# A causal convolution's taps held in program order, fewer of them among the projections, and a normalization row one chunk later

## The chip, the cores and the metric

The kernel runs on one core of a Trainium2 chip. The metric is the device time in microseconds (us) of one execution, lower is better. A core has five engines that run their own instruction streams and wait for each other by semaphores: PE (TensorE, matmuls), DVE (VectorE), ACT (ScalarE), POOL (GpSimd) and SP (SyncE, which here only issues DMAs).

## What is computed

A hybrid decoder layer for 256 tokens of width 1024, all in float32: a convolution branch and a sparse-attention branch share one input projection and one output projection; after them come a cross-attention to a memory of 256 tokens, a mixture of 16384 tiny experts chosen by product keys, and a final norm. Cut to what this change touches:

```python
def conformer_conv(a, b, w_dw, b_dw, ln_g, ln_b):
    u = a * jax.nn.sigmoid(b)
    y = lax.conv_general_dilated(      # depthwise, causal, CONV_KERNEL = 31 taps, 512 channels
        u, w_dw[:, None, :], window_strides=(1,), padding=[(CONV_KERNEL - 1, 0)], ...)
    y = layernorm(y + b_dw, ln_g, ln_b)
    return jax.nn.silu(y)

hn = rmsnorm(h, mix_norm_g[l])
proj = hn @ w_in[l]
conv_a, conv_b, q, k_c, v_c, k_s, v_s, k_w, v_w, gate_logits = jnp.split(proj, IN_SPLITS, axis=-1)
y_conv = conformer_conv(conv_a, conv_b, ...)
y_nsa = nsa_mixer(q, k_c, v_c, k_s, v_s, k_w, v_w, gate_logits, ...)
h = h + jnp.concatenate([y_conv, y_nsa], axis=-1) @ w_out[l]
```

## The kernel before

Activations lie transposed, features on 128 partitions and the 256 tokens along the free dimension. A weight chunk of 128 output features is one 512 KB DMA (`raw`, four buffers), which ACT rounds to a coarse part `hi` and DVE turns into a rest `lo` (line 138, two halves of 512 columns, six buffers of each). `proj` then does three matmuls for each of the eight blocks of 128 input features (lines 148 to 150): 24 matmuls of 256 columns for a chunk.

The start of the program is a chain of such chunks: four pairs `pb`, `pa` for the convolution's gate and value (`i` from 0 to 3), two `pkv`, six `pq`, and four double chunks `pv` that hold the values and gates. Before a projection can be used it has to be multiplied by the first norm's row `rs_x`: `r0.sums()` adds squares on PE and DVE takes the reciprocal root, `r0.rows()` spreads it over the partitions by a matmul (`sr_x`, line 224) that ACT copies. `conv_in(i, ...)` forms the gated input `u` of channel group `i` and puts that group's 31 taps on a list; `conv(n)` takes up to `n` of them off it and issues them. A tap is one DVE instruction that adds `u`, shifted by `j`, times a weight to `yc` (line 273; `j` = 0 is line 271): 124 taps in all, and within a group each reads what the last one wrote.

After the projections PE runs the memory's key and value projections as filler, first with the small network that compresses keys (`ph`), then between the 16 units of attention (loop over `n` from 0 to 17). A unit `n` is: scores `pss` on PE, row maximum `amx` on DVE (line 562), exponential on ACT, scaling on DVE, and two units later transposes on PE. Behind the transposes of each `n` stands `conv(6)`. At `n` = 12 `ln_mean()` issues what taps are left and adds the four groups (`lsum`, lines 610 to 613); at `n` = 13 `ln_center` has PE spread the sum (`pmu`, line 619); at 15 and 16 the layernorm's own reciprocal root follows (`ss_c`, `sr_c`). The first two chunks of the output projection are split around there too.

What sets the order: PE's stream is written by hand (`manual_schedule`), so it runs in the order of the code and a matmul that waits holds up all that stand behind it. The streams of DVE, ACT, POOL and SP are ordered by the framework's scheduler at build time, by readiness and place in the program; on the chip each engine then runs its stream strictly in that order.

Of the kernel before, what the change touches and what calls it, by code (L numbers as in the profile page):

```python
# [16 lines left out]
ALU = mybir.AluOpType  # L17
# [4 lines left out]
T = 256  # L22
D = 1024
KC = 8
# [68 lines left out]
def build(tc, A, out, dbg=None):  # L93
    nc = tc.nc
    V, S, G, PE = nc.vector, nc.scalar, nc.gpsimd, nc.tensor
# [17 lines left out]
    def Pm(name):  # L113
        return par[:, PC[name][0]:PC[name][1]]
# [5 lines left out]
    def wload(src, n=1024):  # L120
        cnt[0] += 1
        raw = wts.tile([P, 1024], F32, name=f"raw{cnt[0]}", tag="raw", bufs=4)
        if cnt[0] == 1:
            nc.sync.dma_start(raw[:, 0:512], src[:, 0:512])
            nc.sync.dma_start(raw[:, 512:], src[:, 512:])
        else:
            nc.sync.dma_start(raw[:, 0:n], src)
        return raw, cnt[0]

    def wsplit(w, engs=None, width=P, half=512):  # L130
        raw, i = w
        out_ = []
        for q in range(2):
            hi = wts.tile([P, 512], F32R, name=f"hi{i}{q}", tag="hi", bufs=6)[:, 0:half]
            lo = wts.tile([P, 512], F32R, name=f"lo{i}{q}", tag="lo", bufs=6)[:, 0:half]
            r = raw[:, half * q:half * q + half]
            S.activation(hi, r, AF.Copy)  # L137
            (engs or (V, V))[q].tensor_sub(lo, r, hi.bitcast(F32))  # L138
            for j in range(half // width):
                out_.append((hi[:, j * width:(j + 1) * width], lo[:, j * width:(j + 1) * width]))  # L140
        return out_

    def wchunk(src, engs=None, width=P):

        return wsplit(wload(src), engs, width)

    def mm3(ps, w, xh, xl, start, stop):
        PE.matmul(ps, w[0], xh, start=start, stop=False)  # L148
        PE.matmul(ps, w[0], xl, start=False, stop=False)  # L149
        PE.matmul(ps, w[1], xh, start=False, stop=stop)  # L150

    def proj(ps, w, x, ks=range(KC)):
        for k in ks:
            mm3(ps, w[k], x[0][:, k], x[1][:, k], k == 0, k == KC - 1)
# [20 lines left out]
    def psum(w, name, tag="mm"):  # L175
        return pm.tile([P, 512], F32, name=name, tag=tag, bufs=4)[:, :w]
# [70 lines left out]
    hx = (hx_h, hx_l)  # L247
# [11 lines left out]
    u = ch.tile([P, 4, 30 + T], F32, name="u")  # L259
    V.memset(u[:, :, 0:30], 0.0)  # L260
    yc = ch.tile([P, 4, T], F32, name="yc")
    taps = []

    def conv(n):
        for _ in range(min(n, len(taps))):
            taps.pop(0)()

    def tap(i, j):
        w = Pm("conv_w")[:, i * TAPS + j:i * TAPS + j + 1]
        if j == 0:  # L270
            V.tensor_scalar(yc[:, i], u[:, i, 0:T], w, Pm("conv_b")[:, i:i + 1], op0=ALU.mult, op1=ALU.add)
        else:
            V.scalar_tensor_tensor(yc[:, i], u[:, i, j:j + T], w, yc[:, i], op0=ALU.mult, op1=ALU.add)  # L273

    def conv_in(i, pb, pa):
        tb = wk.tile([P, T], F32, name=f"tb{i}", tag="tb")
        V.tensor_mul(tb, pb, r0.row)
        th = wk.tile([P, T], F32, name=f"th{i}", tag="th")
        S.activation(th, tb, AF.Tanh, scale=0.5)
        ta = wk.tile([P, T], F32, name=f"ta{i}", tag="ta")  # L280
        V.scalar_tensor_tensor(ta, pa, 0.5, r0.row, op0=ALU.mult, op1=ALU.mult)
        V.scalar_tensor_tensor(u[:, i, 30:], th, 1.0, ta, op0=ALU.add, op1=ALU.mult)
        for j in range(TAPS):
            taps.append(lambda j=j: tap(i, j))

    pend = []
    for i in range(4):
        pb = psum(T, f"pb{i}")
        wb = wchunk(A["w_in_t"][2 * i]) if i else w0
        proj(pb, wb, hx, range(4))  # L290
        if i == 1:
            r0.sums()
        proj(pb, wb, hx, range(4, KC))
        wa = wchunk(A["w_in_t"][2 * i + 1], None)
        if i == 0:
            for k in range(KC):
                r0.add(xT[:, k])
            nc.sync.dma_start(con1, A["con"][:, 0:NCON1])
        pa = psum(T, f"pa{i}")
        proj(pa, wa, hx, range(6))  # L300
        if i == 1:
            r0.rows()
            conv_in(*pend)
        proj(pa, wa, hx, range(6, KC))
        if i == 0:
            pend = (i, pb, pa)
        else:
            conv_in(i, pb, pa)
        conv(6)
    nc.sync.dma_start(con2, A["con"][:, NCON1:])  # L310
    posi = wk.tile([P, T], I32, name="posi", tag="rt")
    nc.sync.dma_start(posi, A["pos"].partition_broadcast(P))
# [31 lines left out]
    for i in range(2):  # L344
        G.memset(KV[i], 0.0)
        ps = psum(T, f"pkv{i}")
        proj(ps, wchunk(A["w_in_t"][8 + i]), hx)
        kvT = wk.tile([P, T], F32, name=f"kvT{i}", tag="kvT")
        V.tensor_mul(kvT, ps, r0.row)
        kt = KV[i]  # L350
        S.activation(kt[0:64, 0, 0:T], kvT[0:64, :], AF.Copy)
        S.activation(kt[64:128, 1, 0:T - 1], kvT[64:128, 1:T], AF.Copy)
        nc.sync.dma_start(kt[64:128, 0, 0:T - 1], kvT[0:64, 1:T])
        nc.sync.dma_start(kt[0:64, 1, 0:T], kvT[64:128, :])
        V.tensor_copy(kt[:, 2, 0:32:2], Pm("cmp_pos")[:, 16 * i:16 * i + 16])
        conv(3)
    nc.sync.dma_start(w2, A["w2"])

    w1 = [mp.tile([P, 16, P], F32, name=f"w1_{i}", tag=f"w1_{i}") for i in range(2)]
# [17 lines left out]
    def rope(i, src):  # L377
        pp_ = psum(T, f"rp{i}", "at")
        PE.matmul(pp_, C("perm"), src, start=True, stop=True)
        t = wk.tile([P, T], F32, name=f"rt{i}", tag="rt")  # L380
        V.tensor_mul(t, src, Ct)
        t2 = wk.tile([P, T], F32, name=f"ru{i}", tag="ta")
        V.tensor_mul(t2, pp_, St)
        V.tensor_add(t, t, t2)
        show(f"rope{i}", t)
        dh, dl = (k_h[:, i], k_l[:, i]) if i < 2 else (q_h[:, i - 2], q_l[:, i - 2])
        S.activation(dh, t, AF.Copy)
        V.tensor_sub(dl, t, dh.bitcast(F32))

    todo = []  # L390
    for i in range(6):
        dst = kraw[i] if i < 2 else qraw[:, i - 2]
        ps = psum(T, f"pq{i}")
        proj(ps, wchunk(A["w_in_t"][10 + i]), hx)
        V.tensor_mul(dst, ps, r0.row)
        if i >= 2:
            nc.sync.dma_start(w1[i // 2 - 1][:, 8 * (i % 2):8 * (i % 2) + 8], A["w1"][i // 2 - 1, :, 8 * (i % 2):8 * (i % 2) + 8])
        if i == 1:
            rm.sums()
        todo.append((i, dst))  # L400
        if i > 1:
            rope(*todo.pop(0))
        conv(3)


    vn = ch.tile([P, 2, 256], F32, name="vn")
# [1 line left out]
    for w in range(4):  # L408
        wc = wsplit(wload(A["w_in_v"][w], 560), (V, V), 280, 280)
        for j in range(2):  # L410
            k = 2 * w + j
            for hf in range(2):
                sl = slice(hf * P, (hf + 1) * P)
                PE.matmul(pv[hf], hx_h[:, k, sl], wc[j][0], start=(k == 0), stop=False)
                PE.matmul(pv[hf], hx_h[:, k, sl], wc[j][1], start=False, stop=False)
                PE.matmul(pv[hf], hx_l[:, k, sl], wc[j][0], start=False, stop=(k == KC - 1))
        if w % 2:
            rope(*todo[w // 2])
        if w == 1:
            rm.rows()  # L420
        conv(3)
    gate = ch.tile([P, 2, 8, 3], F32, name="gate")
    chalf = wk.tile([P, 2], F32, name="chalf", tag="bcol")
    V.tensor_scalar(chalf, r0.col, 0.5, None, op0=ALU.mult)
# [40 lines left out]
    def fill(n):  # L465
        for _ in range(n):
            if next(fl, 0) == 0:
                return
# [166 lines left out]
    for n in range(18):  # L635
        if n < 16:
            scores(*units[n])
        if n == 17:
            wc0 = wchunk(A["w_out"][0])
        fill(7 if n < 4 else 5 if n < 14 else 6)  # L640
        if n == 0:
            cmp_keys()
        if n == 1:
            cmp_values()
            cmp_scores(0)
        if n == 2:
            cmp_scores(1)
            prs = psum(512, "prsel", "at")
            for k in range(4):
                PE.matmul(prs[:, k * P:(k + 1) * P], C("rsel")[0:64, k * P:(k + 1) * P], vc2, start=True, stop=True)  # L650
            V.tensor_copy(vcp, prs.rearrange("p (a b) -> p a b", a=4))
        if n in (4, 5):
            cmp_transpose(n - 4)
        if n >= 6 and (n - 6) % 4 == 0:
            weighted((n - 6) // 4)
        if n >= 2:
            transposes(*units[n - 2])
        conv(6)
        if n == 12:
            lsum = ln_mean()  # L660
        if n == 13:
            ln_center(lsum)
        if n == 15:
            rc.sums()
        if n == 16:
            rc.rows()
            ln_out()
# [358 lines left out]
    i, ng = J, 0  # L1026
# [145 lines left out]
```

## Time and profile before

| what | value |
|---|---|
| median of 3 runs | 1117.01 us (1116.13 to 1117.02) |
| the profiled execution | 1117.35 us, of which the span of its instructions is 1115.6 us |
| PE busy | 1069.5 us, 96% of the span |
| DVE busy | 882.1 us, 79% |
| ACT busy | 590.1 us, 53% |
| mean granted clock of PE | 0.983 of full speed |
| the 120 taps of line 273 | 56.0 us busy, 478 ns each |
| PE in the chain that ended last | 87%; DVE 5% |

The sum of the prediction is made against the profiled execution; it lies 0.34 us above the median. An engine's busy time is an average over stages with different limits, so what follows goes by stage: the projections (until 85 us), the compression and the attention's loop (until about 189 us), and the rest, which the change does not touch.

### The profile page before, as it was taken

The page shows a single profiled execution, that of the slowest core. Times are in us where ns is not written, and L with a number is a line of the kernel's source. Part 1 is how long each engine was busy: PE and PEld are TensorE (multiplying, and loading weights), DVE is VectorE, ACT ScalarE, POOL GpSimd, SP SyncE. Part 2 cuts the span into 40 slices and gives each one's busy share as a digit, 9 for nine tenths or more (in the row PEclk, how much of TensorE's full clock was granted, in tenths as well). Part 3 has the DMA queues.
Part 4 walks back from the last instruction along what each step waited for, and adds up shares of the span by engine and source line. Part 5 has one row for each costly group of instructions (what it writes and reads, how often), then busy time and mean ns, then how long its engine had stood idle before and what let it go on. Part 6 is the DMA issues. An engine that isn't in the chain of part 4 may idle for free.

```text
span 1115.6 us, 20623 instructions
## 1 busy us (share of the span) xinstructions
PE 1069.5 (96%) x7362; PEld 980.5 (88%) x7362; DVE 882.1 (79%) x2229; ACT 590.1 (53%) x1354; POOL 111.2 (10%) x86
## 2 busy tenths in 40 slices
PE   8889999999999849999999999999999999999997
PEld 7878778999999749999999999998888888888885
DVE  7998857988789995788899999996666666666665
ACT  5722456666446335566555555455555555555554
POOL 0000000000037749300000000000000000000000
PEclk9899999999999969999999999999999999999999
DMA  8633224625434415644545454456555556665662
GB/s 279 201 107 103 76 95 139 219 97 171 153 114 151 152 57 189 194 164 154 170 155 167 155 170 163 160 170 209 189 195 196 193 190 193 199 193 191 194 198 80
DMA packets 51687, 182.47 MB, mean 164 GB/s; under 512 B 5760, under 2 KB 6528, under 8 KB 51456
## 3 DMA queue, kind: packets, MB, share of 16 engines
q1 hardware_dynamic: 51296, 180.62, 49.8%
q8 instruction: 58, 0.95, 0.3%
q10 hardware_dynamic: 288, 0.52, 0.1%
q14 instruction: 45, 0.37, 0.1%
HBM read 179.81 MB, written 1.05 MB: 162 GB/s over the span
## 4 chain that ended last, share of the span: by engine, by line
PE 87%; DVE 5%; issue 4%; POOL 2%; ACT 2%; DMA 0%; SPq 0%; POOLq 0%; ACTq 0%; DVEq 0%
PE Y L1072 31%; PE pu L148 10%; PE pu L150 10%; PE pu L149 10%; PE pmk L442 3%; POOL lo L138 2%; PE pmv L458 2%; PE pw L1018 1%; PE ppq L148 1%; PE ppq L149 1%; PE ppq L150 1%; PE pw L1019 1%; DVE lo L138 1%; PE pmw L149 1%; PE pmw L148 1%
## 5 line engine op out<-in xcount | busy, mean ns | idle before, releaser
L137 ACT ACTIVATE hi<-raw 128x512 fp32r<-128x512 f32 x632 | 379.2, 623 | 175.8 <-PE pu L149 61.5
L138 DVE TENSOR_TENSOR lo<-raw,hi 128x512 fp32r<-128x512 f32 (+1 forms) x560 | 370.4, 683 | 26.3 <-ACT hi L137 20.0
L148 PE MATMUL pu<-hn_h,hi 128*128 128x256 f32 x1024 | 296.3, 289 | 18.2 <-ACT hi L137 18.2
L150 PE MATMUL pu<-hn_h,lo 128*128 128x256 f32 x1024 | 291.7, 285 | 2.7 <-POOL lo L138 2.7
L149 PE MATMUL pu<-hn_l,hi 128*128 128x256 f32 x1024 | 290.2, 283 | 0.0
L148 PEld LDWEIGHTS pu<-hn_h,hi 128*128 128x128 f32 x1024 | 197.0, 192 | 18.4 <-ACT hi L137 18.4
L150 PEld LDWEIGHTS pu<-hn_h,lo 128*128 128x128 f32 x1024 | 196.7, 192 | 5.3 <-POOL lo L138 5.1
L149 PEld LDWEIGHTS pu<-hn_l,hi 128*128 128x128 f32 x1024 | 197.1, 193 | 0.0
L1072 PE MATMUL Y<-hi,al 128*128 128x512 f32 x512 | 158.1, 389 | 0.0
L1072 PE MATMUL Y<-hi,ah 128*128 128x512 f32 x512 | 158.1, 389 | 0.0
L1072 PE MATMUL Y<-lo,ah 128*128 128x512 f32 x512 | 158.0, 389 | 0.0
L1072 PEld LDWEIGHTS Y<-hi,al 128*128 128x128 f32 x512 | 96.1, 188 | 19.9
L1072 PEld LDWEIGHTS Y<-lo,ah 128*128 128x128 f32 x512 | 96.1, 188 | 19.9
L1072 PEld LDWEIGHTS Y<-hi,ah 128*128 128x128 f32 x512 | 96.0, 188 | 20.0
L158 DVE TENSOR_TENSOR al<-slB,ah 128x256 fp32r<-128x256 f32 x92 | 39.1, 425 | 89.9 <-PE Y L1072 89.9
L138 POOL TENSOR_TENSOR lo<-raw,hi 128x512 fp32r<-128x512 f32 x72 | 103.7, 1476 | 36.5 <-ACT hi L137 36.4
L157 ACT ACTIVATE ah<-slB 128x256 fp32r<-128x256 f32 x92 | 38.5, 418 | 115.7 <-PE Y L1072 115.7
L1024 ACT ACTIVATE slB<-pw 128x364 f32<-128x364 f32 (+31 forms) x64 | 33.4, 522 | 64.7 <-DVE slB L1023 54.2
L273 DVE SCALAR_TENSOR_TENSOR yc<-u,par,yc 128x256 f32<-128x256 f32 x120 | 56.0, 478 | 0.3
L158 DVE TENSOR_TENSOR al<-slA,ah 128x256 fp32r<-128x256 f32 x36 | 15.3, 425 | 33.6 <-PE Y L1072 33.6
L1012 DVE TENSOR_TENSOR o<-iota,i1T 128x512 f16<-128x512 f16 x64 | 28.6, 448 | 12.7 <-ACT i1T L976 12.7
L157 ACT ACTIVATE ah<-slA 128x256 fp32r<-128x256 f32 x36 | 15.0, 418 | 44.1 <-PE Y L1072 43.0
(387 smaller groups left out, 1786.7 us busy)
## 6 DMA issues: line engine op xcount, KB each, us to landing
raw<-u SPq DMA_DIRECT2D x128, 512.0 KB, 3.4
raw<-v SPq DMA_DIRECT2D x128, 512.0 KB, 4.3
raw<-peer_w_q SPq DMA_DIRECT2D x16, 512.0 KB, 3.3
raw<-w_in_t SPq DMA_DIRECT2D x15, 512.0 KB, 4.3
raw<-w_mem_k SPq DMA_DIRECT2D x8, 512.0 KB, 3.4
raw<-w_mem_v SPq DMA_DIRECT2D x8, 512.0 KB, 3.4
raw<-w_out SPq DMA_DIRECT2D x8, 512.0 KB, 3.5
raw<-w_mem_q SPq DMA_DIRECT2D x8, 512.0 KB, 4.3
```

Of the source, the lines that this page charges most:

```text
L137: S.activation(hi, r, AF.Copy)
L138: (engs or (V, V))[q].tensor_sub(lo, r, hi.bitcast(F32))
L148: PE.matmul(ps, w[0], xh, start=start, stop=False)
L149: PE.matmul(ps, w[0], xl, start=False, stop=False)
L150: PE.matmul(ps, w[1], xh, start=False, stop=stop)
L157: S.activation(dst[0], src, AF.Copy)
L158: V.tensor_sub(dst[1], src, dst[0].bitcast(F32))
L273: V.scalar_tensor_tensor(yc[:, i], u[:, i, j:j + T], w, yc[:, i], op0=ALU.mult, op1=ALU.add)
L442: PE.matmul(ps, wr[:, k * P:(k + 1) * P], mg[:, k], start=(k == 0), stop=(k == KC - 1))
L1012: V.tensor_tensor(o1, i4, over_i(i1T), op=ALU.is_equal)
L1024: S.activation(slB[:, done - J:, n0:n0 + 4].rearrange("p i n -> p n i"), pw[:, :, done:], AF.Copy, scale=1.0 / GSC)
L1072: PE.matmul(Y[nh][c], lhs[:, sl], wc[c][t], start=False, stop=i == KEYS - 1 and lhs is a[1], skip_group_check=True)
```

## The change

Four edits, all in `build`. Each tap gets `tc.keep_in_program_order(t)`, which puts it, in DVE's stream, behind the DVE instruction that was issued just ahead of it in the code; it says nothing of which later instructions may be put ahead of the tap. The first norm's row is formed at `i` = 2 instead of 1, so that groups 0 and 1 wait for it together, and `pb0` and `pa0` are held in the other ring of PSUM buffers (tag `at`) meanwhile. Fewer taps are issued by the projections' loops: 4 instead of 6 for a pair, 2 instead of 3 for each later chunk. The attention's loop issues 7 instead of 6.

```diff
--- before.py
+++ after.py
@@ -268,9 +268,10 @@
     def tap(i, j):
         w = Pm("conv_w")[:, i * TAPS + j:i * TAPS + j + 1]
         if j == 0:
-            V.tensor_scalar(yc[:, i], u[:, i, 0:T], w, Pm("conv_b")[:, i:i + 1], op0=ALU.mult, op1=ALU.add)
+            t = V.tensor_scalar(yc[:, i], u[:, i, 0:T], w, Pm("conv_b")[:, i:i + 1], op0=ALU.mult, op1=ALU.add)
         else:
-            V.scalar_tensor_tensor(yc[:, i], u[:, i, j:j + T], w, yc[:, i], op0=ALU.mult, op1=ALU.add)
+            t = V.scalar_tensor_tensor(yc[:, i], u[:, i, j:j + T], w, yc[:, i], op0=ALU.mult, op1=ALU.add)
+        tc.keep_in_program_order(t)
 
     def conv_in(i, pb, pa):
         tb = wk.tile([P, T], F32, name=f"tb{i}", tag="tb")
@@ -285,7 +286,7 @@
 
     pend = []
     for i in range(4):
-        pb = psum(T, f"pb{i}")
+        pb = psum(T, f"pb{i}", "mm" if i else "at")
         wb = wchunk(A["w_in_t"][2 * i]) if i else w0
         proj(pb, wb, hx, range(4))
         if i == 1:
@@ -296,17 +297,18 @@
             for k in range(KC):
                 r0.add(xT[:, k])
             nc.sync.dma_start(con1, A["con"][:, 0:NCON1])
-        pa = psum(T, f"pa{i}")
-        proj(pa, wa, hx, range(6))
-        if i == 1:
+        pa = psum(T, f"pa{i}", "mm" if i else "at")
+        proj(pa, wa, hx, range(4))
+        if i == 2:
             r0.rows()
-            conv_in(*pend)
-        proj(pa, wa, hx, range(6, KC))
-        if i == 0:
-            pend = (i, pb, pa)
+            for p in pend:
+                conv_in(*p)
+        proj(pa, wa, hx, range(4, KC))
+        if i < 2:
+            pend.append((i, pb, pa))
         else:
             conv_in(i, pb, pa)
-        conv(6)
+        conv(4)
     nc.sync.dma_start(con2, A["con"][:, NCON1:])
     posi = wk.tile([P, T], I32, name="posi", tag="rt")
     nc.sync.dma_start(posi, A["pos"].partition_broadcast(P))
@@ -353,7 +355,7 @@
         nc.sync.dma_start(kt[64:128, 0, 0:T - 1], kvT[0:64, 1:T])
         nc.sync.dma_start(kt[0:64, 1, 0:T], kvT[64:128, :])
         V.tensor_copy(kt[:, 2, 0:32:2], Pm("cmp_pos")[:, 16 * i:16 * i + 16])
-        conv(3)
+        conv(2)
     nc.sync.dma_start(w2, A["w2"])
 
     w1 = [mp.tile([P, 16, P], F32, name=f"w1_{i}", tag=f"w1_{i}") for i in range(2)]
@@ -400,7 +402,7 @@
         todo.append((i, dst))
         if i > 1:
             rope(*todo.pop(0))
-        conv(3)
+        conv(2)
 
 
     vn = ch.tile([P, 2, 256], F32, name="vn")
@@ -418,7 +420,7 @@
             rope(*todo[w // 2])
         if w == 1:
             rm.rows()
-        conv(3)
+        conv(2)
     gate = ch.tile([P, 2, 8, 3], F32, name="gate")
     chalf = wk.tile([P, 2], F32, name="chalf", tag="bcol")
     V.tensor_scalar(chalf, r0.col, 0.5, None, op0=ALU.mult)
@@ -655,7 +657,7 @@
             weighted((n - 6) // 4)
         if n >= 2:
             transposes(*units[n - 2])
-        conv(6)
+        conv(7)
         if n == 12:
             lsum = ln_mean()
         if n == 13:
```

The instructions are the same as before in number and shape (but for the split of two merged rows on SP); the change moves them.

Two places in DVE's stream, and one in PE's, as the build has them. `lo70`, `lo71` are the two halves of the seventh chunk's rest (`pb3`), `lo80`, `lo81` those of `pa3`, `lo90`, `lo91` those of `pkv0`; `tb`, `ta`, `th` and `u` belong to `conv_in`; the digits behind `amx`, `asm`, `ape` are pair, key group and token half (`301` is unit 13).

PE, the first norm's row. A piece of the difference; the matmuls around it are those of `pa1`:

```order
 L149 MATMUL pa1_298<-hx_l_118,hi41_294 128x256
 L150 MATMUL pa1_298<-hx_h_117,lo41_295 128x256
-L224 MATMUL sr_x_317<-dg_x_273,ones_65 128x128 x2
 L148 MATMUL pa1_298<-hx_h_117,hi41_294 128x256
 L149 MATMUL pa1_298<-hx_l_118,hi41_294 128x256
```

The row's matmuls leave this place; they now stand behind the first four blocks of `pa2`, that is 42 matmuls later (6 of `pa1`, 24 of `pb2`, 12 of `pa2`).

DVE, the start of the convolution's input. Before:

```order
L545 CAST causb_1232<-con2_91 128x128
L277 TENSOR_TENSOR tb0_322<-pb0_147,rs_x_320 128x256
L281 SCALAR_TENSOR_TENSOR ta0_326<-pa0_205,rs_x_320 128x256
L277 TENSOR_TENSOR tb1_335<-pb1_230,rs_x_320 128x256
L282 SCALAR_TENSOR_TENSOR u_144<-th0_324,ta0_326 128x256
L281 SCALAR_TENSOR_TENSOR ta1_339<-pa1_298,rs_x_320 128x256
L271 TENSOR_SCALAR yc_146<-u_144,par_64 128x256
```

Now:

```order
L547 CAST causb_1210<-con2_91 128x128
L138 TENSOR_TENSOR lo80_461<-raw8_458,hi80_460 128x512
L138 TENSOR_TENSOR lo81_465<-raw8_458,hi81_464 128x512
L138 TENSOR_TENSOR lo90_536<-raw9_533,hi90_535 128x512
L278 TENSOR_TENSOR tb0_386<-pb0_147,rs_x_384 128x256
L282 SCALAR_TENSOR_TENSOR ta0_390<-pa0_205,rs_x_384 128x256
L278 TENSOR_TENSOR tb1_393<-pb1_230,rs_x_384 128x256
```

Three splits that stood behind `tb0` now stand ahead of it, as does a fourth, `lo71`, a few rows higher. Between `tb0` and the last split of the projections (`lo201`) there stood 51 taps; now 27 do. Up to the first row of the memory's keys (`mkt0`) it was 60, now 32.

DVE, from the row maximum of unit 13 to the mean's sum. Before, all 124 taps and `lsum` stand ahead of this place:

```order
L562 TENSOR_REDUCE amx301_1813<-pss301_1807 128x2
L563 TENSOR_SCALAR amx301_1813<-amx301_1813 128x2
L568 RECIPROCAL asm301_1817<-asm301_1817 128x2
L569 TENSOR_TENSOR asm301_1817<-asm301_1817,gate_1103 128x2
L574 TENSOR_SCALAR ape301_1816<-ape301_1816,asm301_1817 128x256 x2
L621 SCALAR_TENSOR_TENSOR yc_146<-pmu_1838,yc_146 128x256 x4
```

Now 26 taps stand between that maximum and `lsum`; 9 of them come ahead of these rows, among the rows of units 12 and 13, and the other 17 are in them:

```order
L138 TENSOR_TENSOR lo370_2002<-raw37_1999,hi370_2001 128x512
L273 SCALAR_TENSOR_TENSOR yc_146<-u_144,par_64,yc_146 128x256
L138 TENSOR_TENSOR lo371_2006<-raw37_1999,hi371_2005 128x512
L273 SCALAR_TENSOR_TENSOR yc_146<-u_144,par_64,yc_146 128x256 x9
L138 TENSOR_TENSOR lo380_2031<-raw38_2028,hi380_2030 128x512
L273 SCALAR_TENSOR_TENSOR yc_146<-u_144,par_64,yc_146 128x256
L138 TENSOR_TENSOR lo381_2035<-raw38_2028,hi381_2034 128x512
L273 SCALAR_TENSOR_TENSOR yc_146<-u_144,par_64,yc_146 128x256 x6
L614 TENSOR_TENSOR lsum2_1804<-yc_146 128x256
L615 TENSOR_TENSOR lsum_1802<-lsum_1802,lsum2_1804 128x256
```

The splits of the first two chunks of the output projection (`lo370` to `lo381`), which stood behind `pmu`, moved ahead of the sum with them. PE's stream is unchanged there: scores of unit 13, five filler steps, the transposes of unit 11, then `pmu`.


## Rows read from the trace of the kernel before

**Rows 1.** Page, part 1: busy time, share of the span and instructions of PE and DVE.

```profile
PE 1069.5 (96%) x7362; PEld 980.5 (88%) x7362; DVE 882.1 (79%) x2229; ACT 590.1 (53%) x1354; POOL 111.2 (10%) x86
```

**Rows 2.** Windows by stage: us, then busy us (instructions) of PE, PEld, DVE, ACT, POOL; clock, DMA.

```profile
20.80:84.87 64.07, 52.92 (x370) 50.70 (x369) 58.99 (x166) 30.76 (x67) 0.00 (x0) 0.89 0.53 171
24.60:83.60 59.00, 49.83 (x352) 47.86 (x352) 55.37 (x152) 29.66 (x62) 0.00 (x0) 0.90 0.51 166
85.00:162.30 77.30, 77.30 (x436) 63.41 (x435) 57.88 (x195) 28.96 (x105) 0.00 (x0) 1.00 0.27 89
```

**Rows 3.** Waits of PE from 20 to 85 us: us in total, times, longest.

```profile
PE pkv L150 <- DVE lo L138: 4.6, 1, 4.6
PE pq L150 <- DVE lo L138: 2.4, 2, 2.0
PE pv L415 <- DVE lo L138: 2.1, 4, 1.0
PE sr_x L224 <- DVE dg_x L218: 2.0, 1, 2.0
```

**Rows 4.** Timeline of PE at the first norm's row: start us, us, engine, line, operation.

```profile
20.79 0.28 PE L150 MATMUL pa<-hx_h,lo 128*128 128x256 f32 x1
23.05 1.12 PE L224 MATMUL sr_x<-dg_x,ones 128*128 128x128 f32 x4 [1.98 <-DVE dg_x L218]
```

**Rows 5.** Timeline of DVE: start of the gated part, two weight splits, last split; then PE's first filler.

```profile
24.62 0.42 DVE L277 TENSOR_TENSOR tb<-pb,rs_x 128x256 f32<-128x256 f32 x1 [0.93 <-ACT rs_x L226]
44.53 1.28 DVE L138 TENSOR_TENSOR lo<-raw,hi 128x512 fp32r<-128x512 f32 x2
83.18 0.44 DVE L138 TENSOR_TENSOR lo<-raw,hi 128x280 fp32r<-128x280 f32 x1
84.87 5.34 PE L442 MATMUL pmk<-mg,raw 128*128 128x256 f32 x24
```

**Rows 6.** Timeline of PE after two long waits, one of the projections and a later one.

```profile
45.27 0.58 PE L150 MATMUL pkv<-hx_h,lo 128*128 128x256 f32 x1 [4.63 <-DVE lo L138]
48.42 0.41 PE L149 MATMUL pkv<-hx_l,hi 128*128 128x256 f32 x1
48.63 0.41 PE L150 MATMUL pkv<-hx_h,lo 128*128 128x256 f32 x1
50.77 0.28 PE L149 MATMUL pq<-hx_l,hi 128*128 128x256 f32 x1
50.89 0.28 PE L150 MATMUL pq<-hx_h,lo 128*128 128x256 f32 x1
403.94 0.58 PE L148 MATMUL pu<-hn_h,hi 128*128 128x256 f32 x1 [18.20 <-ACT hi L137]
408.85 0.31 PE L148 MATMUL pu<-hn_h,hi 128*128 128x256 f32 x1
```

**Rows 7.** Timeline of DVE: three taps of two channel groups, three of one, two sums.

```profile
110.49 1.27 DVE L273 SCALAR_TENSOR_TENSOR yc<-u,par,yc 128x256 f32<-128x256 f32 x3
135.36 1.53 DVE L273 SCALAR_TENSOR_TENSOR yc<-u,par,yc 128x256 f32<-128x256 f32 x3
144.15 0.40 DVE L612 TENSOR_TENSOR lsum<-yc 128x256 f32<-128x256 f32 x1
144.59 0.43 DVE L613 TENSOR_TENSOR lsum<-lsum,lsum 128x256 f32<-128x256 f32 x1
```

**Rows 8.** Timeline of PE and DVE around attention unit 13 and the layernorm's mean.

```profile
164.75 0.60 PE L619 MATMUL pmu<-lsum,ones 128*128 128x256 f32 x2
162.30 0.69 DVE L562 TENSOR_REDUCE amx<-pss 128x2 f32<-128x512 f32 x1 [1.62 <-PE pss L560]
164.74 0.62 DVE L574 TENSOR_SCALAR ape<-ape,asm 128x256 f32<-128x256 f32 x2
```

**Rows 9.** Waits of PE from 162 to 206 us.

```profile
PE sr_c L224 <- DVE dg_c L218: 1.0, 1, 1.0
```

**Rows 10.** Page, part 6: loads of the output projection's weights.

```profile
raw<-w_out SPq DMA_DIRECT2D x8, 512.0 KB, 3.5
```

## Prediction, made before the changed kernel was run

> **What bounds the kernel now.** I read the page first, then the stages, then what PE waits for in each. On the page PE is busy 96% of the span and DVE 79% [rows 1], so over the whole program PE sets the time; only where PE waits, or runs at the lower clock, is there something to win or lose. The windows [rows 2] show where. From 20.80 to 84.87 us (the projections) PE is busy 52.92 of 64.07 us at a granted clock of 0.89, while DVE is busy 58.99: this stage is DVE's. From 85.00 to 162.30 us (compression and attention up to unit 13) PE has no idle time, and DVE is busy 57.88 of 77.30 us: this stage is PE's, and DVE has 19.4 us free. PE's waits of the first stage [rows 3] add up to 4.6 + 2.4 + 2.1 + 2.0 = 11.1 us, all for DVE. The last of them is the first norm's row: PE is through with its matmuls at 21 us and starts the row at 23.05 [rows 4]. [...]
>
> **The projections.** They end when DVE has made the last weight split, so DVE's stream from the first `tb` (24.62 us) to that split (83.18 us) [rows 5] is to be re-counted.
> - Start: the 42 matmuls that now run ahead of the row take 42 x 0.12 = 5.0 us from 20.8, so PE reaches it at 25.8 instead of 23.05. It finds its input there (DVE had it ready by 23.05, plus one split of 0.60), so the 1.98 us wait is gone and the row itself runs at the full clock, about 0.4 us shorter. `tb` starts some 2.4 us later.
> - Four splits now stand ahead of `tb`, in time that DVE waits for the row anyway. A split costs 0.60 us (two in 1.28, the last one 0.68) [rows 5], so 2.4 us leave the stretch. Start and splits cancel.
> - 51 taps become 27. A tap among other work costs 0.40 us: three in a row of which neighbours belong to different groups take 1.27, the last of them 0.47 [rows 7]. 24 x 0.40 = 9.5 us leave (0.395 each).
> - DVE is idle 59.00 - 55.37 = 3.6 us in this stretch [rows 2], mostly for results of PE, some of them at half clock. I expect half a microsecond less of it.
>
> Gain: 10.0 us, so that the first filler matmul `pmk` starts near 75 instead of 84.87 [rows 5]. Bounds: 5.9 if DVE's idle time doubles for want of taps to fill it; 16.9 if every wait of PE (11.1) and all its slow clock (0.11 x 52.92 = 5.8) went. I stay near the low end, since the longest wait has another cause: the rotation's angles, the two `kvT` and the second norm's sums still stand ahead of a chunk's split. It moves on by one chunk, from the second `pkv` to the first `pq`, at about 4 us.
>
> At no cost I count: `pb0` and `pa0` in the other PSUM ring (`pb3` may wait 0.5 us for `pb1`'s buffer until `tb1` has run; the 4 us wait behind it swallows that, else it costs 0.5), the loads of `w1` that SP now issues one or two chunks later (PE reads them only after the first 12 fillers, 5 us into the next stage), and the pin itself, which adds no instruction.
>
> **The attention's loop.** The 28 taps that left the stretch up to the first `mkt` are to be done here, and DVE has room. The order decides where. In DVE's stream 26 taps stand between unit 13's row maximum and `lsum`. That maximum needs unit 13's scores from PE, so none of the 26 can be early. On PE only 164.75 - 162.30 = 2.45 us of work lies between these scores and `pmu` [rows 8], which needs `lsum`; everything behind `pmu` stands still with it. The price of the pile:
> - The 26 taps are one chain now, each reading what the last wrote. Three taps of one group take 1.53 us with 0.47 for the last, so 0.53 each [rows 7]; 26 x 0.525 = 13.65.
> - The maximum ahead of them 0.61 (0.69 busy, the next starts within it).
> - Four splits between taps: 0.60 + 0.395 - 0.525 = 0.47 each, 1.9.
> - Two scalings of 0.26 (0.62 for two) [rows 8] add 0.13 each, 0.25. The small instructions hide in the chain.
> - The two sums of `lsum`, 0.40 and 0.43 [rows 7], 0.9 with the hand-over.
>
> That is 17.3 us against 2.45: PE waits 14.85 us for the mean. The second chunk's weights are loaded into the buffer that the first one leaves, 3.5 us [rows 10] and a rounding on ACT, under nine taps of 4.7 us; I count nothing for it, and up to 1 if it comes late. Bounds: 26 x 0.395 gives 13.9 in all and a wait of 11.45; with the late load, 15.85.
>
> **After the mean.** The nearest wait in length is a later one of 18.20 us; behind it PE runs at half speed from 403.94 to 408.85 us [rows 6], 4.9 us, and behind the 4.63 us wait it was 5.2 us. I take 5.2 x (1 - 0.12/0.21) = 2.2 us lost. Bounds: half and twice that, 1.1 and 4.4, for the matmuls here are others. Against that, six splits no longer stand behind `pmu`, the last three between `ss_c` and `sr_c`, and the 1.0 us that PE waits for `dg_c` [rows 9] goes: -1.0, at worst 0. It is PE's only wait there, so nothing more is to be had.
>
> **Sum:** -10.0 + 14.85 + 2.2 - 1.0 = +6.05 us. Against the profiled execution's own 1117.35 us (its span of 1115.6 and what lies around it) that is 1123.4; the median of the runs shown lies 0.34 lower, so I forecast 1123.1.
>
> [...] Chained taps cost 0.53 us and unchained ones 0.40 [rows 7]. [...]
>
> **Rivals.**
> - *The free time takes the taps* (0.08, faster). If the pile were worked off before unit 13, the 28 taps, 28 x 0.395 = 11.1 us, would fit into the 19.4 us that DVE has free [rows 2]: gain 10.0, no wait, no slow clock, -1.0 at `sr_c`, 1106.0. [...] For it speaks the free time; against it the built order, in which 26 taps stand behind a maximum that PE sets. The point that decides is how many taps stand there: with the gain and the clock as above the sum is zero at a wait of 8.8 us, which is some 14 taps.
> - *About even* (0.13). Taps at 0.395 though chained (wait 11.45), and PE also freed in the projections, gain 13.5 of the 16.9: -13.5 + 11.45 + 1.7 - 1.0 = -1.35, 1115.7. For it: PE's waits there are all for DVE. Against: rows 7, and the wait that only moves by one chunk.
> - *Little gain ahead, full loss behind* (0.07). DVE, with fewer taps to fill in, idles for PE instead: gain 6, no gain at `sr_c`: -6 + 14.85 + 2.2 = +11, 1128.
>
> **How the numbers follow.** The forecast has 0.72, with its own range of 1119.4 to 1126.5 (gain 8 to 13, wait 13 to 16, clock 1.2 to 3.5, taken together as independent). The range 1117.3 to 1126.5 reaches into the even case; the faster rival, most of the slow one and part of the even one stay outside. About 0.2%, 2.2 us, is what a measurement can tell from no change: faster than 1114.8 gets the first rival and a little of the even one, 0.10; within, most of the even case and the forecast's edge, 0.13; slower 0.77.
>
> **What would show it.** Right: the first `pmk` at 74 to 76 us; no wait for `dg_x`; one wait of some 4 us for a split at the first `pq`; then a wait of 13 to 16 us of `pmu` for `lsum`, with a lower granted clock just behind it, `pmu` near 169.6 us instead of 164.75; no wait for `dg_c`; everything later shifted by the same amount. Wrong: a first `pmk` after 78 or before 72 us (the re-count of DVE), a wait at `pmu` under 11 us (taps cheaper than rows 7 say), or PE waits at `ptt` or `pss` in the attention's loop, of which I count none.

## The result and the profile after

The changed kernel takes 1125.82 us (median of 4, 1125.44 to 1125.93) against 1117.01 us of the kernel before (median of 4): a ratio of 1.0079, interval 1.0062 to 1.0097. The forecast was 1123.1 us, so the sign and the range hold and the size is 2.7 us short. The profiled execution has a span of 1124.2 us, 8.6 more than before.

The page's part 1 for the changed kernel; the totals hardly differ from [rows 1], so nothing was added, it was moved:

```profile
PE 1068.5 (95%) x7361; PEld 980.2 (87%) x7362; DVE 884.3 (79%) x2229; ACT 590.1 (52%) x1354; POOL 111.5 (10%) x86
```

PE's waits in the changed kernel from 15 to 215 us (total us, times, longest):

```profile
PE pmu L621 <- DVE lsum L615: 14.7, 1, 14.7
PE pq L150 <- DVE lo L138: 4.7, 2, 4.2
PE pb L148 <- DVE tb L278: 1.5, 1, 1.5
PE pv L417 <- DVE lo L138: 0.9, 2, 0.5
```

Against [rows 3, 9], the waits for `dg_x` (2.0) and `dg_c` (1.0) are gone, those for splits fell from 9.1 to 5.6, and one of 14.7 us for the mean is new.

Windows of the changed kernel: DVE's stretch from `tb` to the last split, the compression, the wait for the mean, and the time behind it:

```profile
28.80:75.93 47.13, 40.35 (x300) 39.26 (x301) 43.06 (x125) 26.97 (x58) 0.00 (x0) 0.93 0.55 173
85.00:105.00 20.00, 20.00 (x121) 17.35 (x120) 9.97 (x36) 4.56 (x16) 0.00 (x0) 1.00 0.27 81
157.20:171.90 14.70, 0.06 (x1) 0.00 (x0) 14.07 (x33) 3.69 (x9) 0.00 (x0) 0.61 0.31 104
171.99:177.40 5.41, 5.41 (x15) 3.91 (x16) 4.45 (x13) 2.90 (x10) 0.00 (x0) 0.50 0.30 97
177.50:180.00 2.50, 2.50 (x16) 1.86 (x16) 0.00 (x0) 1.48 (x4) 0.00 (x0) 1.00 0.13 21
```

The compression of the kernel before, and the first 20 us of the changed kernel's compression counted from its own first `pmk` (in the kernel before that is nearly the window shown):

```profile
85.00:105.00 20.00, 20.00 (x127) 18.14 (x126) 16.39 (x51) 2.33 (x7) 0.00 (x0) 1.00 0.32 106
```

```profile
77.23:97.23 20.00, 20.00 (x127) 18.15 (x125) 7.09 (x25) 2.46 (x8) 0.00 (x0) 1.00 0.36 107
```

Read them as a story. DVE's stretch shrank from 59.00 us [rows 2] to 47.13, with 125 instructions instead of 152. Then DVE is busy only 9.97 of 20 us in the compression, where it was busy 16.4 before (7.1 against 16.4 if the 20 us are counted from each kernel's own first `pmk`). Then PE stands still for 14.7 us while DVE works through all of it. Then PE runs at half clock (0.50) for some 5.4 us.

PE's timeline of the changed kernel, landmarks (start us, us):

```profile
26.51 0.60 PE L224 MATMUL sr_x<-dg_x,ones 128*128 128x128 f32 x4
...
77.23 1.03 PE L444 MATMUL pmk<-mg,raw 128*128 128x256 f32 x4
...
171.99 1.19 PE L621 MATMUL pmu<-lsum,ones 128*128 128x256 f32 x2 [14.73 <-DVE lsum L615]
...
185.63 0.50 PE L209 MATMUL ss_c<-ones,sa_c 128*128 128x1 f32 x4
...
188.97 0.68 PE L224 MATMUL sr_c<-dg_c,ones 128*128 128x128 f32 x4
```

In the kernel before these stand at 23.05, 84.87, 164.75 [rows 4, 5, 8], 175.74 and 180.16 us:

```profile
175.74 0.50 PE L209 MATMUL ss_c<-ones,sa_c 128*128 128x1 f32 x4
...
180.16 0.68 PE L224 MATMUL sr_c<-dg_c,ones 128*128 128x128 f32 x4 [1.00 <-DVE dg_c L218]
```

So the shift is -7.64 at the first `pmk`, +7.24 at `pmu`, +9.89 at `ss_c`, +8.81 at `sr_c`, and 8.6 at the end. Nothing that matters happens outside these five points.

DVE's timeline of the changed kernel, at the start of the convolution's input and in the pile behind unit 13's maximum:

```profile
28.19 0.69 DVE L138 TENSOR_TENSOR lo<-raw,hi 128x512 fp32r<-128x512 f32 x1 [1.38 <-ACT hi L137]
28.80 0.42 DVE L278 TENSOR_TENSOR tb<-pb,rs_x 128x256 f32<-128x256 f32 x1
...
154.64 0.69 DVE L564 TENSOR_REDUCE amx<-pss 128x2 f32<-128x512 f32 x1
...
161.69 4.64 DVE L273 SCALAR_TENSOR_TENSOR yc<-u,par,yc 128x256 f32<-128x256 f32 x9
...
167.85 3.08 DVE L273 SCALAR_TENSOR_TENSOR yc<-u,par,yc 128x256 f32<-128x256 f32 x6
...
171.42 0.42 DVE L615 TENSOR_TENSOR lsum<-lsum,lsum 128x256 f32<-128x256 f32 x1
```

ACT's timeline ahead of that `tb`, the rounding of the split's chunk and the copy of the norm's row:

```profile
27.53 0.63 ACT L137 ACTIVATE hi<-raw 128x512 fp32r<-128x512 f32 x1 [1.75 <-DMA raw<-w_in_t]
28.07 0.37 ACT L226 ACTIVATE rs_x<-sr_x 128x256 f32<-128x256 f32 x1
```

From 160.09 us on the trace has DVE's rows in the order of the build. From the maximum (154.64) to the end of `lsum` (171.84) DVE needs 17.2 us. The taps of the pile start (4.64 - 0.47) / 8 = 0.521 us apart.

### The profile page after: what moved, and what is told of

Its sections match the earlier page's. It is cut to its first block, busy times and chain, and to the rows that moved or that the text cites. A ratio compares the mean times of both kernels' runs of the same rounds, so it can differ in the third digit from the quotient of the medians.

```text
span 1124.2 us, 20624 instructions
## 1 busy us (share of the span) xinstructions
PE 1068.5 (95%) x7361; PEld 980.2 (87%) x7362; DVE 884.3 (79%) x2229; ACT 590.1 (52%) x1354; POOL 111.5 (10%) x86
## 4 chain that ended last, share of the span: by engine, by line
PE 87%; DVE 5%; issue 3%; POOL 2%; ACT 1%; DMA 1%; SPq 0%; POOLq 0%; DVEq 0%; ACTq 0%
PE Y L1074 31%; PE pu L148 10%; PE pu L150 10%; PE pu L149 10%; PE pmk L444 3%; PE pmv L460 2%; POOL lo L138 2%; DVE yc L273 1%; PE pw L1020 1%; PE ppq L148 1%; PE ppq L149 1%; PE ppq L150 1%; PE pw L1021 1%; DMA raw<-w_in_t 1%; DVE lo L138 1%
```

## The experiments

My theory before the runs: the pin leaves DVE no tap for the compression (between the first `mkt` and the first attention maximum the built order holds none, 24 before), the taps pile up behind unit 13's maximum, and PE stands behind that pile. The rivals were that smaller counts lose by themselves, that a pinned tap is dearer, and that the attention's loop has no room for 28 more taps. Runs that are compared share their runs of the kernel before (medians 1116.74, 1117.87 and 1117.52 us in the three groups), so the ratio with its interval is the figure to compare. "Shift" is how much later than before a landmark stands in the profiled execution.

**1. Without the pin.**

```diff
-        tc.keep_in_program_order(t)
```

> The changed kernel without the pin (the taps are free again; row one chunk later and the smaller counts stay). In the built order 30 taps stand up to the projections' last split instead of 27, all 124 ahead of unit 13's maximum. Theory (the pile of 26 taps behind unit 13 is the whole loss): first pmk 3 x 0.395 = 1.2 us later than in the changed kernel, at 78.4; no wait of pmu; the wait of sr_c of 1.0 us back, since the splits stand behind pmu again: 1117 - 6.4 = 1110.6 us (1109 to 1112). Rival 1 (the attention's loop cannot take 28 more taps, wherever they stand): PE waits in the loop instead, 1117 or more. Rival 2 (the smaller counts lose, not the pin): about 1125 again.

1111.45 us, ratio 0.9949 (0.9935 to 0.9962). First `pmk` at 78.98, no wait of `pmu`, shift -5.9 from there to the end. DVE is busy 15.84 of 20 us in the compression again. Without the pin the two other edits gain: the rivals on smaller counts and on room in the loop fall. PE's timeline, the mean:

```profile
158.44 0.60 PE L585 MATMUL ptt<-con,ape 128*128 128x128 f32 x4
158.88 0.60 PE L620 MATMUL pmu<-lsum,ones 128*128 128x256 f32 x2
```

**2. Pin kept, taps issued in the compression.**

```diff
             if jj % 2:
                 fill(1)
+                conv(2)
```

> The changed kernel, pin and counts kept, with conv(2) added at each of the 16 fillers of the compression's two loops: 20 taps now stand between the first mkt and the first attention maximum, where the changed kernel has none, and none behind unit 13. Theory (the pin shut the taps out of the compression, where DVE is free, and so made the pile): first pmk at 77.2 as in the changed kernel, no wait of pmu, sr_c's 1.0 us wait back: 1117 - 7.6 = 1109.4 us (1108 to 1111). Rival 1 (pinned taps are themselves dear, each bound to its neighbour): the loop still runs late, 1115 or more. Rival 2 (DVE's free time of 19 us is no real room, it is lost between PE's steps): PE waits at pss or ptt, 1115 or more.

1112.15 us, ratio 0.9958 (0.9943 to 0.9972). The first `pmk` came at 76.18, 1.0 us earlier than expected (shift -8.7); 1.4 us of that went in the loop, where PE waited 0.47 us at `pss` and 0.36 at `ptt`, so Rival 2 is there in small. `pmu` without a wait, at 157.44; shift -7.3 there. Window of the compression:

```profile
85.00:105.00 20.00, 20.00 (x124) 17.39 (x122) 16.24 (x55) 4.50 (x16) 0.00 (x0) 1.00 0.27 96
```

DVE is busy 16.24 us where the changed kernel has 9.97. So a pinned tap is as good as a free one where the program has a place for it. The median lies 1.2 us above the expected range; in the profiled execution 1.6 us of the shift go again behind `sr_c`, near 450 us, in code that the change does not touch (see the last section).

**3. The counts of before, pin and later row kept.**

```diff
-        conv(4)
+        conv(6)
...
-        conv(2)
+        conv(3)
...
-        conv(7)
+        conv(6)
```

> The changed kernel with the counts of the kernel before (6, 3, 6), pin and later row kept. 41 taps up to the projections' last split, 12 behind unit 13's maximum, with 2 splits. Theory: first pmk 14 x 0.395 = 5.5 us later than in the changed kernel, 82.8; wait of pmu 14.7 - 14 x 0.52 - 2 x 0.47 = 6.5; clock -2.2: -2.1 + 6.5 + 2.2 - 0.5 = +6.1, 1123 us (1120.5 to 1124.5). Rival (the smaller counts are what loses): no change, 1117, or below.

1125.92 us, ratio 1.0080 (1.0067 to 1.0094): 1.4 us above the range. The wait of `pmu` was 6.51 us, as worked out. What was off is the first `pmk`, 84.53 instead of 82.8. DVE's stretch, this run and then run 5 (which is the same kernel without the pin):

```profile
28.07:83.28 55.21, 43.72 (x302) 42.04 (x301) 48.61 (x139) 27.29 (x58) 0.00 (x0) 0.88 0.45 152
```

```profile
28.94:81.67 52.73, 41.68 (x300) 39.50 (x301) 50.42 (x143) 27.22 (x58) 0.00 (x0) 0.94 0.50 161
```

With the pin DVE idles 55.21 - 48.61 = 6.6 us, without it 2.3. That the pin is the cause is not shown: in the two other pairs of kernels that differ by the pin alone, DVE idles about as much with it as without (3.9 us in run 4 against 3.6 in the kernel before, 4.1 in the changed kernel against 4.6 in run 1).

**4. The pin alone, on the kernel before.**

```diff
+        tc.keep_in_program_order(t)
```

> The kernel before with the pin alone. 46 taps up to the projections' last split instead of 51, 6 behind unit 13's maximum. Theory: first pmk 5 x 0.395 = 2.0 us earlier, 82.9; wait of pmu 14.7 - 20 x 0.52 - 4 x 0.47 = 2.4, clock up to 1.5: -2.0 + 2.4 + 1.5 - 0.5 = +1.4, 1118.4 us (1116.5 to 1120). Rival (a pin adds no instruction and changes nothing by itself): 1117.0. Rival 2 (each pinned tap pays for being bound): 1120 or more, and taps longer than 0.48 us where they stand among others.

1123.69 us, ratio 1.0057 (1.0041 to 1.0072), well above the range. The wait of `pmu` was 2.42 us, as worked out, and the first `pmk` came at 83.44. But PE was slow for longer behind that short wait than behind the long one: its twelve fillers run until 173.2 us, 7.3 us from the start of `pmu`, where the changed kernel has 5.4 us at a granted clock of 0.50. `ss_c` came 3.3 us late for it (14.32 us from `pmu`, 10.99 before):

```profile
165.91 1.15 PE L620 MATMUL pmu<-lsum,ones 128*128 128x256 f32 x2 [2.42 <-DVE lsum L614]
...
168.12 5.12 PE L459 MATMUL pmv<-raw,mg 128*128 128x256 f32 x12
...
177.15 2.81 PE L459 MATMUL pmv<-raw,mg 128*128 128x256 f32 x12
```

Twelve fillers take 5.12 us behind the wait and 2.81 later, a factor of 1.8. Shift +4.5 at `sr_c`; another 2.6 us come between 220 and 460 us, in untouched code. A tap lasts 479 ns on average here and 478 in the kernel before, so rival 2 finds no dearer tap. The pin adds no instruction, and up to `sr_c` it costs by the order that it makes.

**5. The later row alone, on the kernel before.** The edit is that of the change: `r0.rows()` at `i` = 2 after four blocks, `pb0` and `pa0` in the ring `at`.

> The kernel before with the later row alone (and pb0, pa0 in the other ring). 45 taps up to the projections' last split instead of 51, no pile. Theory now (the row's move is no gain, since one of the splits that stand ahead of tb waits for ACT's rounding of its chunk): tb starts 4.2 us later (28.8), four splits (2.4) and six taps (2.4) leave the stretch behind it: first pmk 84.87 + 4.2 - 2.4 - 2.4 = 84.3, time 1117 - 0.6 = 1116.4 us (1115.5 to 1117.5). Rival (the prediction's step: start and splits cancel): first pmk at 82.5, 1114.6 us.

1115.67 us, ratio 0.9981 (0.9972 to 0.9991), that is 2.2 us below the kernel before of its group. `tb` came at 28.94, as my theory had it, but the first `pmk` at 82.96, nearer the rival: DVE idled 2.3 us behind `tb` instead of 3.6. So the row's move is a gain of about 2 us, and my theory on it falls.

**6. The smaller counts alone, on the kernel before.**

```diff
-        conv(6)
+        conv(4)
...
-        conv(3)
+        conv(2)
...
-        conv(6)
+        conv(7)
```

> The kernel before with the smaller counts alone (4, 2, 7), no pin, row as before. 34 taps up to the projections' last split instead of 51, no pile. Theory (taps taken out of the projections are won at 0.395 us each where DVE takes them in the next stages): first pmk 17 x 0.395 = 6.7 us earlier, 78.2; 1110.3 us (1109 to 1111.5), that is as good as without the pin with both other edits. Rival (the row's move is a part of the gain): 1112 or more.

1111.70 us, ratio 0.9945 (0.9932 to 0.9959). That is 0.2 us above the range, but the range was counted from 1117 us, and against the kernel before of its own group the gain is 6.2 of the 6.7 us expected. First `pmk` at 79.46, shift -5.4 to the end. The 17 taps brought 0.32 us each, and DVE's idle time in its stretch rose from 3.6 to 4.8. That is as much as both edits without the pin (run 1).

**7. The last two channel groups in turn**, in the changed kernel.

```diff
+        at = len(taps) - TAPS
         for j in range(TAPS):
-            taps.append(lambda j=j: tap(i, j))
+            taps.insert(at + 2 * j + 1 if i == 3 else len(taps), lambda j=j: tap(i, j))
```

> The changed kernel with the taps of the last two channel groups taken in turn, so that neighbours belong to different groups. The built order has 15 taps and 2 splits behind unit 13's maximum instead of 26 and 4. Theory (a tap costs 0.525 us behind its own group's, 0.395 behind another's): wait of pmu 14.7 - 11 x 0.52 - 2 x 0.47 - 15 x 0.13 = 6.1; first pmk at 77.2; clock -2.6 (1.8 to 3.3 so far): -7.6 + 6.1 + 2.6 - 0.8 = +0.3, 1117.3 us (1116 to 1119). Rival (a tap costs the same either way, the order alone changes): wait 8.1, 1119.3 us; rows of taps in turn would still start 0.52 apart.

1119.75 us, ratio 1.0021 (1.0011 to 1.0030). DVE's timeline, seven taps in turn:

```profile
147.74 2.85 DVE L273 SCALAR_TENSOR_TENSOR yc<-u,par,yc 128x256 f32<-128x256 f32 x7
```

The median lies 0.75 us above the range. The taps start (2.85 - 0.47) / 6 = 0.397 us apart, where the changed kernel's chained ones start 0.521 apart. This shows the price. The wait was 8.29 us instead of 6.1, though, which is what the rival gave, and not for its reason: behind the maximum DVE also waited 0.5 us for a rounding of ACT, and the rest, some 1.7 us, lies in the small instructions and scalings between the taps, which a chain's gaps had hidden. That last part is read off the timeline and was not tried by itself.

**8. Counts of 3, 1 and 6, on the kernel before.**

```diff
-        conv(6)
+        conv(3)
...
-        conv(3)
+        conv(1)
```

> The kernel before with counts of 3, 1 and 6, no pin, row as before. 20 taps up to the projections' last split instead of 51, 54 up to the first attention maximum instead of 84, none behind unit 13's. Theory (DVE has 19.4 us free between 85 and 162 us, 31 taps need 12.2): first pmk at 72.6 to 73.5, no new wait in the loop: 1105.5 us (1104 to 1107.5). Rival (the loop is near its limit, as two waits of 0.4 us in the run with taps in the compression hint): PE waits at pss or ptt and some at pmu, 1108 to 1112.

1108.77 us, ratio 0.9918 (0.9904 to 0.9931), 1.3 us above the range, and the first `pmk` came some 3 us later than expected. Shift -8.55 from the first `pmk` (76.33) to the end, no wait in the loop: the room is there, and the rival falls. But 31 taps brought 0.28 us each, not 0.395. In the stretch from `tb` DVE was busy 42.98 of 48.97 us, so 0.40 a tap did leave (55.39 - 42.98 = 12.4), and 2.4 came back as idle time. Of the other 1.5 us, 0.9 is no price of a tap: `tb` started at 25.49 us in this execution, 0.87 later than before, though the order ahead of it is that of before. DVE's waits from 25 to 75 us:

```profile
DVE sa_m L202 <- ACT sq_m L201: 1.9, 1, 1.9
DVE kraw L395 <- PE pq L150: 1.6, 1, 1.6
DVE St L339 <- ACT St L335: 1.3, 1, 1.3
```

These are waits of other work; of the three the kernel before has only the last, with 0.3 us. That the taps which used to stand ahead of them gave ACT and PE the time is my reading of it and was not tried by itself.

**9. The later row with counts of 3, 1 and 6**, no pin, `conv(3)` in the compression: the changed kernel with these edits.

> The changed kernel without the pin and with counts of 3, 1 and 6 and conv(3) at the compression's fillers: the later row joined to the counts that were best. 17 taps up to the projections' last split, none behind unit 13's maximum. Theory (a tap taken out of the projections is worth some 0.28 to 0.30 us at this end, because DVE then idles more; the later row adds its 1.9 us less what the six taps it took out were worth): first pmk at 75.0 to 75.6, 1107.0 to 1108.0 us, at most 1.5 below the run with counts of 3, 1 and 6. Rival (both gains add up in full): 8.55 + 1.9 = 10.5 us, 1106.5 us or below.

1107.18 us, ratio 0.9907 (0.9891 to 0.9923), inside the range by luck. Against the kernel before of its own group the gain is 10.3 us, so the time alone does not exclude the rival's 10.5. The first `pmk` came at 72.72 (shift -12.2, more than even the rival), because DVE idled 3.2 us and not 6. Then 2.6 us went in the loop (shift -9.55 at `sr_c`): behind a wait of 0.47 us PE ran at a granted clock of 0.70 from 108.4 to 114.1. The profiled execution was the slowest of the five (1110.08 us) and ends only 7.3 us early; the last 2.3 us went behind `sr_c`, a part of them near 450 us as in run 2.

**10. No tap issued in the projections**, `conv(4)` in the compression, the mean one unit later, no pin, row as before.

> The kernel before with no tap issued in the projections' loops, conv(4) at the compression's fillers, and the mean one unit later, no pin, row as before: 15 taps (put there by the scheduler) up to the projections' last split instead of 20 with counts of 3, 1 and 6. Theory (DVE's waits for ACT and PE take over, with fewer taps to fill them): DVE's idle time in the stretch 6 us or more, first pmk 0.5 to 1.5 us earlier than with 3, 1 and 6 counted from tb; 1107 to 1109 us, no new wait in the attention's loop. Rival (each tap is still worth 0.395): 2.0 us less, 1106.5 or below.

1108.11 us, ratio 0.9915 (0.9898 to 0.9932). Again the first `pmk` came earlier than expected, at 71.26, with DVE idle 3.3 us, and a part went in the loop, again with a wait of 0.47 us at `pss` (shift -13.6 at the first `pmk`, -10.3 at `ss_c`, -10.1 at the end). My theory that idle time grows as taps go falls with this run: over all ten runs it lies between 2.3 and 6.6 us without following the number of taps.

Runs 1, 2, 5, 6 and 8 to 10 beat both kernels, the last three by most. The intervals of these three overlap, so none is shown to be the best of them; run 8 has the smallest edit, two counts of the kernel before (the second at three places).

## Why the prediction was right, and where it was off

**The wait for the mean: right.** 14.85 us forecast, 14.73 measured, and 17.2 us of DVE's work against 17.3 worked out. The terms carry over: the same prices, counted down from 14.7 us, gave 6.5 and 2.4 us for the piles of runs 3 and 4, and 6.51 and 2.42 were measured. That the pile is the cause is shown by run 2, which keeps pin, counts and row and takes only the pile away.

**The chained tap: right.** 0.525 us forecast, 0.521 measured in the pile, and 0.397 where two groups take turns (run 7). The measurement decides against the bound in which both cost the same (26 x 0.395, a wait of 11.45 us). The taps in turn start 0.397 us apart and last 0.47, so each starts 0.07 us before the one ahead of it has ended; the chained ones start 0.05 us behind its end.

**The projections: direction right, size off.** Forecast -10.0, measured -7.64. The failed step is "Start and splits cancel". DVE's busy time in its stretch fell as costed (55.39 to 43.06 us, 12.3 against the 11.9 of 9.5 + 2.4). But `tb` started 4.2 us later, not 2.4. PE reached the row at 26.51 us instead of 25.8, in part by scatter: where the row is not moved, PE reaches it at 23.05 us before and at 23.11 to 24.08 in runs 4, 6, 8 and 10. And a split that now stands ahead of `tb` waited 1.38 us for its rounding on ACT. I had placed that split "in time that DVE waits for the row anyway" and had not asked whether its own input was there: the rounding had waited 1.75 us for the load of its chunk, and ACT's copy of the row stood behind it, so that the row was copied at 28.07 to 28.44 although PE was done with it at 27.11. Without the split `tb` could have come 0.36 us earlier; the larger part lies in ACT's queue, which I had not looked at. The rest is DVE's idle time, which I had fall by 0.5 us and which rose from 3.6 to 4.1. Sum: 1.8 + 1.0 - 0.4 = 2.4. By the shift of the first `pmk` a tap that goes was worth 0.32 and 0.28 us in runs 6 and 8, not 0.395; by DVE's stretch from `tb` alone, net of the idle time that opens, 0.33 and 0.32.

**The clock: right in kind.** 2.2 us forecast, 2.65 measured (`pmu` to `ss_c` 13.64 us instead of 10.99), inside the bounds of 1.1 to 4.4. The forecast took its 5.2 us and the ratio 0.12/0.21 from the matmuls behind the 4.63 us wait [rows 6]; the windows of the kernel before give the granted clock of the two stretches, 0.50 and then 1.00:

```profile
45.27:50.50 5.23, 5.23 (x24) 5.23 (x25) 4.74 (x12) 3.28 (x8) 0.00 (x0) 0.50 0.33 100
50.50:52.00 1.50, 1.50 (x15) 1.50 (x14) 1.50 (x5) 1.46 (x5) 0.00 (x0) 1.00 0.94 243
```

Behind `pmu` the changed kernel has 0.50 from 171.99 to 177.40 us, 5.4 us where 5.2 were taken. The bounds were needed: see below.

**`dg_c`: right.** Its wait is gone, -1.08 us. In runs 1, 2 and 8, where no split stands ahead of the mean's sum behind unit 13's maximum, it is there again with 1.0 us.

**At no cost: one entry off, harmless.** PE waited 1.5 us for `tb` at `pb3`, not 0.5; the wait of 4.17 us at the first `pq` follows it in a stage that is DVE's.

Sum of the measured terms: -7.64 + 14.73 + 2.65 - 1.08 = +8.66, against a span 8.6 us longer. The rival in which the free time takes the taps was wrong for this kernel, but it is what happens once the pin is off (run 1) or the compression issues taps (run 2): DVE's free time was real, and the taps, once pinned, had no place in it.

What stays open: why DVE's idle time in the projections changes by some 4 us between orders, which I could not foretell from counts, and what sets the length of the half clock.

## What to carry to other kernels

An order that ties work to its place in the program only uses the idle time for which the program has a place: before pinning, list the stages where that engine is free and see whether the new order puts anything there. What counts is not the number of instructions moved but how many stand behind the last input that another engine delivers and ahead of the result that it waits for; multiply that number by the price in just that arrangement (here a chained tap cost 0.521 us, one in turn 0.397), and the wait may come out to a few tenths of a microsecond: 14.73 us against 14.85, 6.51 against 6.5 and 2.42 against 2.4 did, 8.29 against 6.1 in run 7 did not. And when a filler is taken out of a busy stream, look at what it had been filling: in run 8, 2.4 of 12.4 us came back as idle time. An instruction that is moved ahead of another brings the wait for its own input with it, as the split ahead of `tb` did: 1.38 us on DVE, and 1.75 us on ACT, which makes that input.

## What the runs showed of the hardware

**The half clock did not follow the length of the wait.** Behind waits of 2.4, 6.5, 8.3 and 14.7 us at `pmu` (runs 4, 3, 7 and the changed kernel) the way from `pmu` to `ss_c` took 3.3, 1.8, 2.6 and 2.65 us longer than the 10.99 before. In run 9 a granted clock of 0.70 (108.36 to 114.10 us) followed a wait of 0.47 us; in the changed kernel the clock was 1.00 behind a wait of 0.48 us (66.64 to 69.20 us) and behind one of 1.49 us (30.03 to 36.00). A short wait was therefore not cheap by its length, and not always dear.

**One DVE instruction took 11.31 us while POOL worked.** In the untouched stage near 450 us, POOL runs splits one behind the other. In the pin-only run a one-hot instruction of DVE took 11.31 us: it began while POOL was at a split (450.15 us) and ended 0.3 us behind the last of them (461.46 against 461.18). The second of the pair ended 0.34 us later, and the next one-hot instruction (461.73 us), behind POOL's last split, took 0.41. The first alone, and the pair:

```profile
450.15 11.31 DVE L1013 TENSOR_TENSOR o<-iota,i1T 128x512 f16<-128x512 f16 x1 [12.66 <-ACT i1T L977]
```

```profile
450.15 11.65 DVE L1013 TENSOR_TENSOR o<-iota,i1T 128x512 f16<-128x512 f16 x2 [12.66 <-ACT i1T L977]
```

POOL in that run:

```profile
442.36 18.82 POOL L138 TENSOR_TENSOR lo<-raw,hi 128x512 fp32r<-128x512 f32 x15
```

In the kernel before the same pair took 2.75 us, and POOL was at its splits there too:

```profile
444.58 2.75 DVE L1012 TENSOR_TENSOR o<-iota,i1T 128x512 f16<-128x512 f16 x2 [12.65 <-ACT i1T L976]
```

```profile
441.81 15.11 POOL L138 TENSOR_TENSOR lo<-raw,hi 128x512 fp32r<-128x512 f32 x11
```

There the two took 1.31 and 1.51 us, and each ended 0.3 us behind the end of the split that POOL was at when it began (445.89 against 445.60 us, 447.32 against 447.05). What decides between the two ways is not shown. In run 9, where the pair took 11.64 us, PE then waits 1.38 us (447.98 us) for what is queued behind the pair; the kernel before has no wait of PE at that place. The long form appears in the profiled executions of runs 2, 3, 4, 7 and 9 (11.64 to 11.68 us for the pair), and not in those of the others (2.72 to 2.75), so it explains part of the distance between a run's shift at `sr_c` and its end.
